# Seven-product output projection: combinations, row transfers and next-layer splits placed step by step, a third pair of split weights

## Chip, cores and metric

One core of one Trainium2 chip runs the whole program. The metric is the device time of one execution in microseconds (us), as a median over runs; lower is better.

## What is computed

A decoder trunk of two layers on 512 positions and 2048 channels, in float32. Each layer normalises x, projects it by `w_in` into the inputs of three groups (a state-space group, a convolution group, a differential attention), gates their outputs and projects them back:

```python
y = jnp.concatenate([y_ssd, y_cfm, y_att], axis=-1)
x = x + jnp.einsum("bse,ed->bsd", y, w_out[l])
```

The change lies in the second line of each layer, in how `x` is handed to the next layer, and in the buffers that serve both.

## The kernel before

Every large matmul is made of three on numbers that are split in two: a weight tile `w` of 128 x 1024 is copied by ACT into a short format (`wh`, line 141) and DVE subtracts that from `w` (`wl`, line 142); activations are split likewise into hi and lo. TensorE then adds hi*wh, hi*wl and lo*wh into a PSUM bank. `weights` (line 130) does this for each weight tile. The pool `wsp` holds two pairs of `wh` and `wl`, so the split of a tile waits until TensorE has ended with the tile two before it.

The output projection of a layer has two halves. Output channels 0 to 1023 come from two calls of `project` (line 815), 8 weight tiles each, 24 matmuls to a tile. Output channels 1024 to 2047 come from seven products (`product`, line 859), a scheme that saves the eighth product of a 2 x 2 split of the matrices and pays with sums: of activations (`s_make`, line 788, done before), of weights (`w_add` and `w_less`, lines 846 and 854, one DVE instruction of 128 x 1024 to a tile), and of results (`each`, line 890, DVE instructions of 128 x 512).

Each product has four **steps**; this text numbers them 0 to 27 in a layer, so product 1 is steps 0 to 3 and product 7 steps 24 to 27. A step loads one weight tile of 512 KB by SP (`load`, line 831: four buffers in turn, two of the pool `wraw` and the tags `vA` and `vB`), sums it into one of four running tiles `wsum` where the product asks for a sum (products 2, 3, 5 and 7), splits it and runs 12 matmuls of 512 columns. The results of a product lie in two PSUM tiles: `pa` (products 1 and 6), `pc` (2 and 4), `pb` (3, 5 and 7).

The four groups of output rows `r22`, `r12`, `r21` and `r11`, two tiles of 128 x 512 each, start as rows of x that POOL loads from memory (`x_rows`, line 885), and gather the products: r22 takes p1 (a copy of `pa` after product 1, line 928), `pc` after product 2 and `pb` after product 5; r12 takes p1, `pb` after product 3 and `pc` after product 4; r21 takes p1 and, last, `pb` after product 7; r11 takes `pa` after product 6. `done` (line 908) stores them.

In the first layer the next layer's activations are made beside the products. Channels 0 to 1023 of the new x are read back from memory by `again` (line 915: POOL loads, eight tiles of 256 KB); the rows of the products are transposed by TensorE and copied by ACT (`turn`, line 897). `put_x` (line 120) then scales and splits a tile (ACT line 117, DVE line 118) and adds its square to a running sum for the normalisation (ACT lines 110 and 113, DVE line 114).

TensorE's order is the order in which the program is written. The order on ACT, DVE, SP and POOL is set by a scheduler at build time, by priority: what stands in `with urgent()` goes before everything, `soon()` before the rest, and `with tc.issue_after(ins)` keeps an instruction behind `ins`. In the kernel before, the weight splits, the sums of weights and the combinations (`each`) are all urgent, and the squares of `again`'s tiles are put wherever the scheduler finds room. On the chip each engine takes its instructions strictly in the order that was so made, and so do the DMA queues.

Of the kernel before, what the change touches and what calls it, by code (L numbers as in the profile page):

```python
# [45 lines left out]
def kernel(  # L46
# [83 lines left out]
    def weights(src, raw=None, between=None):  # L130

        with urgent():
# [3 lines left out]
            h = wsp.tile([P, 2, S], F32R, tag="wh", name="wh")  # L136
            lo = wsp.tile([P, 2, S], F32R, tag="wl", name="wl")
# [92 lines left out]
    def load_x(kk, w):  # L230
# [7 lines left out]
        for j in range(2):  # L238
            k = 2 * kk + j
            if k in (8, 10):  # L240
                xv[0] = big.tile([P, 2, S], F32, tag=("vA", "vB")[(k - 8) // 2], name=f"xraw{k}")
            t = xv[0][:, k % 2, :] if 8 <= k < 12 else big.tile([P, S], F32, tag=f"xs{k}" if k < 8 else f"p{k - 12}", name=f"xraw{k}")
# [30 lines left out]
    for l in range(DEPTH):  # L273
# [43 lines left out]
        else:  # L317
            jobs = late + [lambda: after(1, x_stats), par_load, lam_job]
# [78 lines left out]
        xs = [None] * 8  # L397
# [79 lines left out]
        def conv_x(i, raws, xs=xs, conv4=conv4):  # L477
            xs[i] = big.tile([P, S], F32, tag=f"xs{i}", name=f"xs{i}")
            conv4(raws[i % 4], i, xs[i])
# [245 lines left out]
        def ssd_out(i, xs=xs, ry=ry, yact=yact, col=col, yv=yv):  # L725
            t = wt2()
            V.scalar_tensor_tensor(t, xs[i], col(PP_SN + i), ry[0], ALU.mult, ALU.mult)
            if i in (0, 2):
                yv[0] = big.tile([P, 2, S], F32R, tag=("vA", "vB")[i // 2], name=f"ysh{i}")
            hi = yv[0][:, i % 2, :] if i < 4 else big.tile([P, S], F32R, tag=f"p{i - 4}", name=f"ysh{i}")  # L730
            lo = big.tile([P, S], F32R, tag=f"xs{i}", name=f"ysl{i}")
            split(hi, lo, t)
            yact[i] = (hi, lo)
# [37 lines left out]
        banks = in_proj(CH_CZ, True, mix([ahead(lambda t=t: att_out(t)) for t in range(4)] + [lambda i=i: ssd_out(i) for i in range(8)],  # L771
# [82 lines left out]
        def w_less(s_):  # L854
            raw = load(quarter(0, 0, s_))
            V.tensor_tensor(raw, chain[s_], raw, ALU.subtract)
            return raw

        def product(src, lhs, banks, start, jobs=()):
# [35 lines left out]
        xk = [None] * KB  # L895

        def turn(t, e, c, xk=xk):
# [4 lines left out]
            for b in range(4):  # L902
                k = 8 + 4 * e + b
                if xk[k] is None:
                    xk[k] = big.tile([P, S], F32, tag=f"p{b}", name=f"x1_{k}") if e else rw()
                A.copy(xk[k][:, blk(t)], ps[:, blk(b)])

        def done(tiles, t0, e, l=l):
# [4 lines left out]
            return [lambda n=n: turn(t0 + n, e, tiles[n]) for n in range(2)] if l < DEPTH - 1 else []  # L913
# [5 lines left out]
        nxt = l < DEPTH - 1  # L919
        put = lambda *ks, l=l, xk=xk: [lambda k=k: put_x(l + 1, k, xk[k]) for k in ks] if nxt else []  # L920
        r21 = x_rows([lt([P, S], "rl"), lt([P, S], "rc")], 2, 0)
# [12 lines left out]
        each(ALU.add, r21, r21, p1)  # L934
        product(w_add(1, 1), lambda j, t: part(slab(8 + j), 2 + t), pb, True,
                [lambda k=k: again(k) for k in range(4, 8)] if nxt else [])
        each(ALU.subtract, r12, r12, pb)
        r11 = x_rows([wt2(), wt2()], 0, 0)
        product(lambda s_: load(quarter(1, 1, s_)), lambda j, t: part(slab(j), 2 + t), pc, False)
        each(ALU.subtract, r12, r12, pc)  # L940
        jobs = done(r12, 0, 1)
        product(w_less, lambda j, t: part(slab(j), t), pb, False, [lambda: None] * 2 + jobs)
        each(ALU.subtract, r22, r22, pb)
        jobs = done(r22, 2, 1)
        product(lambda s_: load(quarter(1, 0, s_)), lambda j, t: part(yact[k1(j)], t), pa, False,
                [lambda: None] * 2 + jobs + put(0, 1, 2, 3))
        each(ALU.add, r11, r11, pa)
        jobs = done(r11, 0, 0)
        product(w_add(1, 0), lambda j, t: part(yact[k1(j)], 2 + t), pb, False,
                [lambda: None] * 2 + jobs + put(4, 5, 6, 7))  # L950
        each(ALU.add, r21, r21, pb)
        jobs = done(r21, 2, 0)
# [71 lines left out]
```

## Time and profile before

| what | value |
|---|---|
| median of 3 runs | 1555.08 us (1554.63 to 1555.27) |
| the profiled execution's own time | 1558.73 us |
| its span, first to last instruction | 1557.0 us |
| TensorE (PE) busy | 1530.3 us, 98% |
| DVE busy | 1121.7 us, 72% |
| ACT busy | 747.5 us, 48% |
| POOL busy | 72.8 us, 5% |
| mean granted TensorE clock | 0.996 |

The profiled execution is 3.65 us above the median of the runs. "Busy" of PE counts a matmul until its modelled end, so PE is nearly always busy in it; what a stretch of matmuls loses shows in their starts, which follow each other at a constant pace as long as nothing is waited for.

### The profile page before, as it was taken

Reading aid. Unit: us, or ns where it says so; the run is one execution under the profiler, and the core shown is the slowest. Engines: PE = TensorE matmul, PEld = TensorE weight load, DVE = VectorE, ACT = ScalarE, POOL = GpSimd, SP = SyncE. Lnnn points to the kernel's source line nnn. Section 1 sums busy time; section 2 is a strip of 40 time slices with the busy share of each in tenths; the row PEclk is TensorE's granted clock in tenths of the full one; section 3 lists DMA queues with packets and bytes.
Section 4 is the critical chain, followed back from the end, with each engine's and each line's share of the span. In section 5 each row is a group of like instructions: output and inputs, shape, how many; then the busy total and the mean of one; then the engine's idle time right before and its main releaser. Section 6 shows DMA issues by size and latency. Waiting matters only on the chain.

```text
span 1557.0 us, 18864 instructions
## 1 busy us (share of the span) xinstructions
PE 1530.3 (98%) x7156; PEld 1244.8 (80%) x7156; DVE 1121.7 (72%) x1741; ACT 747.5 (48%) x1173; POOL 72.8 (5%) x136
## 2 busy tenths in 40 slices
PE   9999999999999999998999999999999999999988
PEld 6778888888888888876677788888888888888866
DVE  7654646988688889837856546469886888898475
ACT  6433727333475556323645328273334755563232
POOL 0010100000000000111000101100000000000000
PEclk9999999999999999998999999999999999999999
DMA  7253443333322333445632534332333223345455
GB/s 243 82 144 89 119 118 100 87 97 93 95 81 77 114 118 119 149 159 174 211 101 82 141 92 119 118 100 82 95 95 95 81 74 108 121 118 159 162 158 157
DMA packets 55196, 184.10 MB, mean 118 GB/s; under 512 B 7776, under 2 KB 8672, under 8 KB 55104
## 3 DMA queue, kind: packets, MB, share of 16 engines
q1 hardware_dynamic: 46112, 156.34, 33.2%
q0 software_dynamic: 8992, 26.55, 5.6%
q8 instruction: 56, 0.92, 0.2%
q14 instruction: 36, 0.29, 0.1%
HBM read 174.40 MB, written 8.45 MB: 117 GB/s over the span
## 4 chain that ended last, share of the span: by engine, by line
PE 87%; DVE 4%; DMA 4%; issue 3%; ACT 1%; POOL 1%; SPq 0%; DVEq 0%; POOLq 0%; ACTq 0%
PE ps_p L190 17%; PE ps_p L192 17%; PE ps_p L191 17%; PE ps_p L196 7%; PE ps_p L194 7%; PE ps_p L195 7%; DVE wl L142 2%; DMA wraw<-w_out 2%; PE ps_p L874 2%; PE ps_p L875 2%; PE ps_p L873 1%; PE ps_s L678 1%; PE ps_s L465 1%; PE ps_s L470 1%; DMA e<-acr 1%
## 5 line engine op out<-in xcount | busy, mean ns | idle before, releaser
L141 ACT ACTIVATE wh<-wraw 128x1024 fp32r<-128x1024 f32 (+1 forms) x249 | 262.3, 1054 | 545.7 <-PE ps_p L191 260.9
L142 DVE TENSOR_TENSOR wl<-wraw,wh 128x1024 fp32r<-128x1024 f32 (+1 forms) x249 | 303.1, 1217 | 225.6 <-ACT wh L141 214.5
L190 PE MATMUL ps_p<-xh,wh 128*128 128x512 f32 x1024 | 413.0, 403 | 4.2 <-DVE rw L330 2.7
L192 PE MATMUL ps_p<-xh,wl 128*128 128x512 f32 x1024 | 400.8, 391 | 0.0
L191 PE MATMUL ps_p<-xl,wh 128*128 128x512 f32 x1024 | 399.9, 391 | 0.0
L190 PEld LDWEIGHTS ps_p<-xh,wh 128*128 128x128 f32 x1024 | 193.1, 189 | 53.9 <-ACT wh L141 5.5
L191 PEld LDWEIGHTS ps_p<-xl,wh 128*128 128x128 f32 x1024 | 193.2, 189 | 41.7 <-issue 3.8
L192 PEld LDWEIGHTS ps_p<-xh,wl 128*128 128x128 f32 x1024 | 192.8, 188 | 41.9 <-DVE wl L142 0.3
L194 PE MATMUL ps_p<-wh,xh 128*128 128x512 f32 x512 | 202.6, 396 | 0.0
L196 PE MATMUL ps_p<-wh,xl 128*128 128x512 f32 x512 | 199.7, 390 | 0.0
L195 PE MATMUL ps_p<-wl,xh 128*128 128x512 f32 x512 | 199.4, 389 | 0.0
L519 DVE SCALAR_TENSOR_TENSOR ca<-u,ppt,ca 128x512 f32<-128x512 f32 x240 | 179.3, 748 | 3.5
L196 PEld LDWEIGHTS ps_p<-wh,xl 128*128 128x128 f32 x512 | 96.1, 188 | 20.4
L194 PEld LDWEIGHTS ps_p<-wh,xh 128*128 128x128 f32 x512 | 96.2, 188 | 19.0
L195 PEld LDWEIGHTS ps_p<-wl,xh 128*128 128x128 f32 x512 | 96.3, 188 | 18.9
L141 ACT ACTIVATE wh<-wsum 128x1024 fp32r<-128x1024 f32 x32 | 34.0, 1061 | 67.7 <-PE ps_p L875 22.3
L142 DVE TENSOR_TENSOR wl<-wsum,wh 128x1024 fp32r<-128x1024 f32 x32 | 39.1, 1222 | 16.5 <-ACT wh L141 16.2
L190 PE MATMUL ps_p<-ysh,wh 128*128 128x512 f32 x128 | 50.8, 396 | 0.0
L191 PE MATMUL ps_p<-ysl,wh 128*128 128x512 f32 x128 | 49.9, 390 | 0.0
L192 PE MATMUL ps_p<-ysh,wl 128*128 128x512 f32 x128 | 49.9, 389 | 0.0
L420 DVE TENSOR_TENSOR xdt<-ps_s,dt 128x512 f32<-128x512 f32 x16 | 11.0, 689 | 45.4 <-PE ps_s L418 45.4
L651 DVE TENSOR_TENSOR ps_s<-ps_s,cst 128x128 f32<-128x128 f32 x64 | 18.3, 295 | 34.7 <-PE ps_s L650 34.3
(529 smaller groups left out, 2219.4 us busy)
## 6 DMA issues: line engine op xcount, KB each, us to landing
wraw<-w_in SPq DMA_DIRECT2D x191, 512.0 KB, 3.6
wraw<-w_out SPq DMA_DIRECT2D x80, 512.0 KB, 3.7
m<-acr POOLq DMA_DIRECT2D x32, 256.0 KB, 4.5
xraw<-xT SPq DMA_DIRECT2D x16, 256.0 KB, 5.0
wsum<-w_out SPq DMA_DIRECT2D x8, 512.0 KB, 3.6
out<-rw SPq DMA_DIRECT2D x12, 256.0 KB, 4.1
wT<-acr POOLq DMA_DIRECT2D x24, 96.0 KB, 4.0
rw<-xT POOLq DMA_DIRECT2D x8, 256.0 KB, 4.2
```

Source lines behind the costliest of these rows:

```text
L141: pace_hi[0] = A.activation(h[:, part, :], raw[:, part, :], AF.Copy).ins
L142: pace[0] = V.tensor_tensor(lo[:, part, :], raw[:, part, :], h[:, part, :].bitcast(F32), ALU.subtract).ins
L190: T.matmul(banks[b], h[:, c], ah, start=first, stop=False)
L191: T.matmul(banks[b], h[:, c], al, start=False, stop=False)
L192: T.matmul(banks[b], lo[:, c], ah, start=False, stop=last)
L194: T.matmul(banks[b], ah[:, c], h, start=first, stop=False)
L195: T.matmul(banks[b], ah[:, c], lo, start=False, stop=False)
L196: T.matmul(banks[b], al[:, c], h, start=False, stop=last)
L519: V.scalar_tensor_tensor(ca[i], u[i][:, j:j + S], w(j), ca[i], ALU.mult, ALU.add)
L651: V.tensor_tensor(ps[:, d0:n], ps[:, d0:n], amask, ALU.add)
L874: T.matmul(banks[t], hi, wl, start=False, stop=False, **again)
L875: T.matmul(banks[t], lo, h, start=False, stop=s_ == 3 and j == 1, **again)
```

## The change

`weights` may place its pair in a third pair of buffers: the tags `xs0` and `xs1`, which hold two tiles of 128 x 512 each now (the eight tags `xs0` to `xs7` become four twice as large, and the code that uses them takes them in pairs: `load_x`, `conv_x`, `ssd_out`, `again`). From step 5 on, every third step uses it, so that a split then waits for the tile three before it. `load` and its four raw buffers are not touched.

The combinations, the row loads, the copy of p1, the transposes and the next layer's splits become jobs of a step. A combination is no longer urgent; it stands behind the newest weight split (`paced`). A sum of weights stands behind the split of two steps before (`before[-2]`). The rows r22 and r12 go into the tags `p0` to `p3` instead of `rw`; the ones that are turned into channels 1536 to 2047 go into `rw` and the others into `p0` to `p3`. Of channels 0 to 1023, tiles 0 to 3 are still put beside the products, tiles 4 to 7 only in the next layer's first projection.

```diff
-    def weights(src, raw=None, between=None):
+    def weights(src, raw=None, between=None, third=False):
...
-            h = wsp.tile([P, 2, S], F32R, tag="wh", name="wh")
-            lo = wsp.tile([P, 2, S], F32R, tag="wl", name="wl")
+            h, lo = [big.tile([P, 2, S], F32R, tag=t3, name=n) if third else wsp.tile([P, 2, S], F32R, tag=n, name=n)
+                     for n, t3 in (("wh", "xs0"), ("wl", "xs1"))]
...
                 raw = load(quarter(q, e, s_))
-                V.tensor_tensor(chain[s_], chain[s_], raw, ALU.add)
+                with tc.issue_after(before[-2]):
+                    V.tensor_tensor(chain[s_], chain[s_], raw, ALU.add)
...
-                wt = weights(None, raw)
+                wt = weights(None, raw, third=steps[0] > 4 and steps[0] % 3 == 2)
+                steps[0] += 1
+                before.append(pace[0])
...
-        def each(op, dst, a, b):
-            with urgent():
-                for n in range(2):
-                    V.tensor_tensor(dst[n], a[n], b[n], op)
+        def each(op, dst, b):
+            for n in range(2):
+                V.tensor_tensor(dst[n], dst[n], b[n], op)
...
-            xk[k] = big.tile([P, S], F32, tag=f"xs{k}", name=f"x1_{k}")
-            G.dma_start(out=xk[k], in_=x1[k])
+            xp = big.tile([P, 2, S], F32, tag=f"xs{(2, 3, 0, 1)[k // 2]}", name=f"x1_{k}")
+            for n in range(2):
+                xk[k + n] = xp[:, n, :]
+                G.dma_start(out=xp[:, n, :], in_=x1[k + n])
...
-        r22 = x_rows([rw(), rw()], 2, 1)
-        r12 = x_rows([rw(), rw()], 0, 1)
-        p1 = [wt2(), wt2()]
-        with urgent():
-            for n in range(2):
-                A.copy(p1[n], pa[n])
-        each(ALU.subtract, r22, r22, p1)
-        product(w_add(0, 1), lambda j, t: part(slab(8 + j), t), pc, True,
-                [lambda k=k: again(k) for k in range(4)] if nxt else [])
-        each(ALU.subtract, r22, r22, pc)
-        each(ALU.subtract, r12, r12, p1)
-        each(ALU.add, r21, r21, p1)
...
+        product(w_add(0, 1), lambda j, t: part(slab(8 + j), t), pc, True, [
+            lambda: rows_in("22", lambda: [ptile(0), ptile(1)], 2, 1), p1_copy, none, op(SUB, "22", "p")])
+        product(w_add(1, 1), lambda j, t: part(slab(8 + j), 2 + t), pb, True, [
+            op(SUB, "22", pc), none, lambda: rows_in("12", lambda: [ptile(2), ptile(3)], 0, 1), none])
+        product(lambda s_: load(quarter(1, 1, s_)), lambda j, t: part(slab(j), 2 + t), pc, False, [
+            op(SUB, "12", pb), op(SUB, "12", "p"), op(ADD, "21", "p"), none])
+        product(w_less, lambda j, t: part(slab(j), t), pb, False, [
+            seq(op(SUB, "12", pc), lambda: done(rows["12"], 0, 1)),
+            lambda: rows_in("11", lambda: [wt2(), wt2()], 0, 0), *turns("12", 0, 1)])
+        product(lambda s_: load(quarter(1, 0, s_)), lambda j, t: part(yact[k1(j)], t), pa, False, [
+            seq(op(SUB, "22", pb), lambda: done(rows["22"], 2, 1), only(lambda: (again(0), again(2)))),
+            none, seq(*turns("22", 2, 1)), only(later(lambda: put(0, 1)))])
+        product(w_add(1, 0), lambda j, t: part(yact[k1(j)], 2 + t), pb, False, [
+            seq(op(ADD, "11", pa), lambda: done(rows["11"], 0, 0)), only(later(lambda: put(2, 3))),
+            *turns("11", 0, 0)])
...
+            late = [lambda again=again: (again(4), again(6)),
+                    lambda tn=tn, put=put: (tn[0](), tn[1](), put(4, 5)),
...
```

What this makes of the order on the engines is shown at three places, all in the first layer. In them `wsum` and `wraw` are the weight tiles that are summed or split, `wl` and `wh` the split pair, `rb` and `sa` the running sum of squares and one square, `x_0` to `x_7` the tiles that `again` reads back, `wT` the copy of p1. Before, DVE's order from the split of step 3 to the combinations ahead of the split of step 7 is:

```order
L142 TENSOR_TENSOR wl<-wsum,wh 128x1024
L114 TENSOR_TENSOR rb<-rb,sa 128x512
L849 TENSOR_TENSOR wsum<-wsum,wraw 128x1024
L142 TENSOR_TENSOR wl<-wsum,wh 128x1024
L893 TENSOR_TENSOR rl<-rl,wT 128x512
L849 TENSOR_TENSOR wsum<-wsum,wraw 128x1024
L893 TENSOR_TENSOR rc<-rc,wT 128x512
L142 TENSOR_TENSOR wl<-wsum,wh 128x1024
L114 TENSOR_TENSOR rb<-rb,sa 128x512
L893 TENSOR_TENSOR rw<-rw,wT 128x512 x2
L142 TENSOR_TENSOR wl<-wsum,wh 128x1024
L893 TENSOR_TENSOR rw<-rw,wT 128x512 x2
```

After the change DVE's order from the split of step 3 through that of step 9 is:

```order
L142 TENSOR_TENSOR wl<-wsum,wh 128x1024
L855 TENSOR_TENSOR wsum<-wsum,wraw 128x1024
L142 TENSOR_TENSOR wl<-wsum,wh 128x1024 x2
L855 TENSOR_TENSOR wsum<-wsum,wraw 128x1024 x2
L142 TENSOR_TENSOR wl<-wsum,wh 128x1024 x2
L855 TENSOR_TENSOR wsum<-wsum,wraw 128x1024 x2
L903 TENSOR_TENSOR rows<-rows,wT 128x512
L142 TENSOR_TENSOR wl<-wsum,wh 128x1024
L855 TENSOR_TENSOR wsum<-wsum,wraw 128x1024
L142 TENSOR_TENSOR wl<-wsum,wh 128x1024
```

All four combinations with the rows that are loaded in product 2 (`rw` before) stood ahead of the splits of steps 6 and 7; now one (`rows`) stands ahead of the split of step 8, and the sums of weights stand two at a time ahead of two splits. ACT's order before, from the splits of steps 0 to 2 on:

```order
L141 ACTIVATE wh<-wsum 128x1024 x3
L110 ACTIVATE rb<-x_0_5710 128x512
L113 ACTIVATE sa<-x_1_5731 128x512
L141 ACTIVATE wh<-wsum 128x1024
L113 ACTIVATE sa<-x_2_5752 128x512
L113 ACTIVATE sa<-x_3_5773 128x512
L141 ACTIVATE wh<-wsum 128x1024
```

and after the change, from the splits of steps 0 to 5 on (`x_0_6039` holds tiles 0 and 1, `x_2_6042` tiles 2 and 3):

```order
L141 ACTIVATE wh<-wsum 128x1024 x6
L950 COPY wT<-ps_p 128x512 x2
L110 ACTIVATE rb<-x_0_6039 128x512
L113 ACTIVATE sa<-x_0_6039 128x512
L141 ACTIVATE wh<-wsum 128x1024 x2
L113 ACTIVATE sa<-x_2_6042 128x512 x2
L141 ACTIVATE wh<-wsum 128x1024 x4
```

The first two squares moved from ahead of the split of step 3 to ahead of the split of step 6, the next two to ahead of the split of step 8, and the squares of tiles 4 to 7 are gone from here. At the end of the first layer's products DVE's order after the change, from the last combination to the split for the second weight tile of the next layer's first projection, is:

```order
L903 TENSOR_TENSOR rl<-rl,ps_p 128x512
L502 MEMSET u_7689 128x30
L118 SCALAR_TENSOR_TENSOR xl_122<-rw,nwt,xh_106 128x512
L903 TENSOR_TENSOR rc<-rc,ps_p 128x512
L502 MEMSET u_7692 128x30
L118 SCALAR_TENSOR_TENSOR xl_113<-x_6_6283,nwt,xh_97 128x512
L142 TENSOR_TENSOR wl<-wraw,wh 128x1024
```

The split of tile 6 of the new x, read back into the buffers of the third pair, now stands ahead of that weight split. On all engines the instructions ahead of the first layer's products, and between the next layer's first projection and its products, stand in the order of before, apart from the names of buffers.

## Rows read from the trace of the kernel before

**Rows 1.** Windows: busy us (and instructions) of PE, PEld, DVE, ACT, POOL; clock, DMA.

```profile
690.00:789.00 99.00, 88.03 (x371) 68.11 (x370) 76.93 (x86) 48.53 (x79) 12.01 (x23) 0.95 0.57 188
1468.00:1553.00 85.00, 79.15 (x338) 62.34 (x336) 60.93 (x61) 29.71 (x29) 3.22 (x6) 1.00 0.58 182
...
717.30:722.80 5.50, 5.50 (x13) 4.34 (x14) 4.46 (x5) 0.49 (x1) 1.07 (x2) 0.50 0.49 141
```

**Rows 2.** Waits of PE: total us, times, longest.

```profile
PE ps_s L874 <- DVE wl L142: 7.8, 5, 3.5
PE ps_p L874 <- DVE wl L142: 5.9, 8, 1.7
```

**Rows 3.** Timeline of PE (start, us): ends of both layers' products, end of product 1.

```profile
690.24 0.40 PE L873 MATMUL ps_p<-wh,ysh 128*128 128x512 f32 x1
...
788.76 0.40 PE L190 MATMUL ps_p<-xh,wh 128*128 128x512 f32 x1
...
1468.12 0.40 PE L873 MATMUL ps_p<-wh,ysh 128*128 128x512 f32 x1
...
1478.81 0.39 PE L875 MATMUL ps_p<-wh,ysl 128*128 128x512 f32 x1
...
1552.28 0.40 PE L875 MATMUL ps_p<-wh,ycl 128*128 128x512 f32 x1
```

**Rows 4.** Timeline of PE, first layer: other work between the products' matmuls.

```profile
706.75 1.07 PE L269 MATMUL ps_s<-rw,wd 128*32 128x512 f32 x8
...
758.48 0.60 PE L901 MATMUL ps_s<-cst,rw 128*128 128x128 f32 x4
758.84 0.48 PE L873 MATMUL ps_p<-wh,xh 128*128 128x512 f32 x1
```

**Rows 5.** Timeline of PE, first layer: the two longest waits.

```profile
701.30 0.50 PE L873 MATMUL ps_p<-wh,ysh 128*128 128x512 f32 x1 [2.70 <-ACT wh L141]
...
717.21 0.80 PE L874 MATMUL ps_s<-wl,xh 128*128 128x512 f32 x1 [3.50 <-DVE wl L142]
```

**Rows 6.** Timeline of ACT, first layer, ahead of the wait at 701.30.

```profile
697.21 0.63 ACT L110 ACTIVATE rb<-x 128x512 f32<-128x512 f32 x1 [2.95 <-DMA x<-x]
699.67 0.63 ACT L113 ACTIVATE sa<-x 128x512 f32<-128x512 f32 x1 [1.83 <-DMA x<-x]
700.20 1.04 ACT L141 ACTIVATE wh<-wsum 128x1024 fp32r<-128x1024 f32 x1
```

**Rows 7.** Timeline of POOL, then of DVE, first layer, ahead of the wait at 717.21.

```profile
708.09 2.12 POOL L887 DMA_DIRECT2D rw<-xr  x4 [0.44 <-PE ps_s L269]
...
714.68 1.34 DVE L893 TENSOR_TENSOR rw<-rw,wT 128x512 f32<-128x512 f32 x2 [4.42 <-issue]
```

**Rows 8.** Timeline of DVE, second layer, steps 4 to 6.

```profile
1478.37 1.23 DVE L849 TENSOR_TENSOR wsum<-wsum,wraw 128x1024 f32<-128x1024 f32 x1 [2.25 <-DMA wraw<-w_out]
...
1480.64 1.89 DVE L893 TENSOR_TENSOR rw<-rw,wT 128x512 f32<-128x512 f32 x3
...
1483.05 1.22 DVE L142 TENSOR_TENSOR wl<-wsum,wh 128x1024 fp32r<-128x1024 f32 x1
```

**Rows 9.** Landing: lines L838 and L917; weight loads issued in 685:720 and 1466:1490.

```profile
DMA to landing us min/median/max: 3.4/4.0/8.9
...
DMA to landing us min/median/max: 3.0/6.2/6.6
...
wraw<-w_out SPq DMA_DIRECT2D x7, 512.0 KB, 6.4
...
wraw<-w_out SPq DMA_DIRECT2D x8, 512.0 KB, 5.2
```

**Rows 10.** Durations (page's groups: busy us, mean ns, idle before; line L849: ns).

```profile
L141 ACT ACTIVATE wh<-wsum 128x1024 fp32r<-128x1024 f32 x32 | 34.0, 1061 | 67.7 <-PE ps_p L875 22.3
L142 DVE TENSOR_TENSOR wl<-wsum,wh 128x1024 fp32r<-128x1024 f32 x32 | 39.1, 1222 | 16.5 <-ACT wh L141 16.2
...
L849 DVE TENSOR_TENSOR wsum<-wsum,wraw x24: 1218/1222/1227, 687.5 to 1543.2; 128x1024 f32<-128x1024 f32 x24
```

More of the change, by code (lines that the diff above doesn't have):

```diff
@@ L317 @@
         else:
-            jobs = late + [lambda: after(1, x_stats), par_load, lam_job]
+            jobs = late + [lambda: (after(1, x_stats), par_load()), lam_job]
         banks = in_proj(CH_BC, True, jobs, first_pre, order=range(KB // 2) if l == 0 else KORD)
@@ L769 @@
             yact[12 + h] = (yah[:, h, :], yal[:, h, :])
-        banks = in_proj(CH_CZ, True, mix([ahead(lambda t=t: att_out(t)) for t in range(4)] + [lambda i=i: ssd_out(i) for i in range(8)],
+        banks = in_proj(CH_CZ, True, mix([ahead(lambda t=t: att_out(t)) for t in range(4)] + [(lambda i=i: ssd_out(i)) if i % 2 == 0 else (lambda: None) for i in range(8)],
                                          tp[6] + [cfm_norm] + [lambda: None] * NPAD))
@@ L855, in w_less @@
             raw = load(quarter(0, 0, s_))
-            V.tensor_tensor(raw, chain[s_], raw, ALU.subtract)
+            with tc.issue_after(before[-2]):
+                V.tensor_tensor(raw, chain[s_], raw, ALU.subtract)
             return raw
+        before, steps = [], [0]
         def product(src, lhs, banks, start, jobs=()):
@@ L888, in x_rows @@
             return tiles
-        def each(op, dst, a, b):
-            with urgent():
-                for n in range(2):
-                    V.tensor_tensor(dst[n], a[n], b[n], op)
+        def each(op, dst, b):
+            for n in range(2):
+                V.tensor_tensor(dst[n], dst[n], b[n], op)
         xk = [None] * KB
+        nxt = l < DEPTH - 1
         def turn(t, e, c, xk=xk):
@@ L904, in turn @@
                 if xk[k] is None:
-                    xk[k] = big.tile([P, S], F32, tag=f"p{b}", name=f"x1_{k}") if e else rw()
-                A.copy(xk[k][:, blk(t)], ps[:, blk(b)])
+                    xk[k] = rw() if e else big.tile([P, S], F32, tag=f"p{b}", name=f"x1_{k}")
+                with tc.issue_after(pace_hi[0]):
+                    A.copy(xk[k][:, blk(t)], ps[:, blk(b)])
         def done(tiles, t0, e, l=l):
@@ L933 @@
-        each(ALU.subtract, r12, r12, p1)
-        each(ALU.add, r21, r21, p1)
[L935 to L952, printed above, removed]
@@ L953 @@
-        if nxt:
-            both = lambda a, b: lambda: (a(), b())
-            pt = put(12, 13, 14, 15, 8, 9, 10, 11)
-            late = [both(pt[0], pt[1]), both(pt[2], pt[3])] + jobs + [
-                lambda xk=xk: (dt_mm(3, xk[12:16], 2), dt_mm(2, xk[8:12], 2)), both(pt[4], pt[5]), both(pt[6], pt[7])]
+            xp = big.tile([P, 2, S], F32, tag=f"xs{(2, 3, 0, 1)[k // 2]}", name=f"x1_{k}")
+            for n in range(2):
+                xk[k + n] = xp[:, n, :]
+                G.dma_start(out=xp[:, n, :], in_=x1[k + n])
@@ new lines, in put, with rows_in, p1_copy @@
+        def put(*ks, l=l, xk=xk):
+            for k in ks:
+                put_x(l + 1, k, xk[k])
+        ptile = lambda n: big.tile([P, S], F32, tag=f"p{n}", name="rows")
+        none = lambda: None
+        later = lambda fn: lambda: paced(fn)
+        only = lambda fn: fn if nxt else none
+        rows = {}
+        def rows_in(key, tiles, t0, e):
+            rows[key] = x_rows(tiles(), t0, e)
+        def p1_copy():
+            rows["p"] = [wt2(), wt2()]
+            with tc.issue_after(pace_hi[0]):
+                for n in range(2):
+                    A.copy(rows["p"][n], pa[n])
@@ new lines @@
+        op = lambda o, key, b: later(lambda: each(o, rows[key], rows[b] if isinstance(b, str) else b))
+        SUB, ADD = ALU.subtract, ALU.add
+        turns = lambda key, t0, e: [only(lambda n=n: turn(t0 + n, e, rows[key][n])) for n in range(2)]
+        seq = lambda *fns: lambda: [fn() for fn in fns]
+        rows_in("21", lambda: [lt([P, S], "rl"), lt([P, S], "rc")], 2, 0)
+        product(w_first, lambda j, t: part(yact[j], t), pa, True, jobs)
+        product(w_add(0, 1), lambda j, t: part(slab(8 + j), t), pc, True, [
+            lambda: rows_in("22", lambda: [ptile(0), ptile(1)], 2, 1), p1_copy, none, op(SUB, "22", "p")])
@@ new lines @@
+        with urgent():
+            each(ADD, rows["21"], pb)
+        done(rows["21"], 2, 0)
+        if nxt:
+            tn = turns("21", 2, 0)
+            late = [lambda again=again: (again(4), again(6)),
+                    lambda tn=tn, put=put: (tn[0](), tn[1](), put(4, 5)),
+                    lambda put=put: put(6, 7, 12, 13), lambda put=put: put(14, 15),
+                    lambda put=put, xk=xk: (dt_mm(3, xk[12:16], 2), dt_mm(2, xk[8:12], 2), put(8, 9)),
+                    lambda put=put: put(10, 11)]
```

32 lines of the change are left out of this document (15 added, 17 removed).

## The prediction

> **What bounds the kernel now.** I read the windows of the two stages first, then the waits of PE, then the starts of its matmuls, and then ACT and DVE ahead of the longest waits. TensorE is the bound nearly everywhere, so a change is worth what it takes out of the time that TensorE loses, and only the two stretches of the seven products are touched in order.
>
> What is lost there follows from starts. In product 1 of the second layer nothing is waited for: from 1468.12 to 1478.81 there are 47 starts, a pace of 0.2274 us [rows 3]. The second layer's products have 335 further starts up to 1552.28, in 84.16 us; at that pace they would take 76.2, so 8.0 us are lost. The first layer's take 98.52 us from 690.24 to the next projection's first matmul at 788.76. Of this 336 starts are 76.4; the eight small matmuls for the next layer's `dt` cost 1.1 and six groups of four transposes 0.36 each, or 2.2 [rows 4]. That leaves 18.8 us lost, and **26.8 us in both layers**.
>
> The waits of PE say where. Most are for `wl`, the DVE half of a weight split: 7.8 and 5.9 us, in 5 and 8 waits [rows 2], and one of 2.70 us for `wh`, the ACT half [rows 5]. The two longest show what an order in advance does to an engine that can't pass anything:
> - Ahead of 701.30 ACT stands at two squares of tiles that are just being read back: 2.95 and 1.83 us idle, released by DMA. The weight split behind them starts at 700.20, and PE, which needs it, has been waiting [rows 6].
> - Ahead of 717.21 POOL issues the row loads at 708.09, and DVE stands 4.42 us at the combination that wants them. What released it is given as issue, but the rows land only then; the weight splits of steps 6 and 7 stand behind [rows 7].
>
> After both, TensorE runs at half clock for a while: 13 matmuls in 5.50 us at a granted 0.50, that is 1.2 GHz, where 13 x 0.2274 = 3.0 would do at 2.4, so 2.5 us more [rows 1]. In the second layer the clock is 1.00 throughout [rows 1] and the same mechanism is short: a sum waits 2.25 us for its weights, then four combinations run ahead of a split [rows 8].
>
> **The change, part by part.**
>
> *Third pair and fixed places.* No arithmetic is added: DVE keeps its 28 splits and 16 sums of 1.22 us and 18 combinations of about 0.69 in each layer [rows 8, 10]. With two pairs a split (1.06 on ACT and 1.22 on DVE, [rows 10]) has one step, 12 x 0.2274 = 2.73 us, between the end of the matmuls that free its buffer and the ones that want it, so a sum of 1.22 beside it leaves 0.3, and any combination makes PE wait. With three pairs it has two steps, 5.46. Since a combination now stands at most one or two at a time between splits, and at a place where its product has ended, all waits behind combinations go, if nothing new comes. I follow the steps in the order that DVE has now and find slack of 2 us or more in products 4 to 7. Products 2 and 3 are the tight ones, since the third pair begins only at step 5 and the loads crowd there.
>
> *Step 6, first layer.* Product 1 begins at 690.24 as before, step 2 ends at 698.4, the product at 701.15, the eight small matmuls at 702.2; so step 6 begins at 707.7 and step 8 at 713.1. Two things gate the split of step 6. On ACT the squares of tiles 0 and 1 now stand ahead of it: their loads go into buffers that step 2 frees, at 698.4, behind two row loads at 0.53 each [rows 7], so about 699.4; landing took 3.0 to 6.6, median 6.2 [rows 9], and I take the median, since eight loads still go together: 705.6. A square (0.63, [rows 6]), the ACT half and the DVE half bring 708.5, with hand-overs 708.8. On DVE the sum of step 7 stands ahead: its load is issued at the end of the sum of step 5, near 699.6, lands 6.4 later (the median of this crowded stretch, [rows 9]) at 706.0, and sum and split make 708.5. PE wants `wl` at 707.9, so it waits **1.0**. Bounds: 0 with a landing of 4.0, 3.4 with one of 8.9 [rows 9].
>
> *Step 8, first layer.* The load of step 9 is issued at 707.3, lands by 712.5 (5.2, as in the second layer's crowd, [rows 9]); sum, one combination and the split end at 715.6, PE wants it at 714.3: **1.3**.
>
> *Second layer.* There are no squares. The sum of step 5 ends near 1477.3; load, sum of step 7 and split of step 6 end at 1477.4 + 5.2 + 1.22 + 1.22 = 1485.1, wanted at 1484.7: **0.4**. The same for steps 9 and 8: 1491.5 against 1490.6: **0.9**.
>
> *Row loads and copies.* r22 and r12 go into buffers that product 1 frees, up to ten us earlier than before, and their combinations stand behind splits; p1's copy stands behind the split of step 5 on ACT. Both are covered by the 5.46 us. If that cover were gone they would cost 0.69 each.
>
> *End of the first layer.* Tiles 4 to 7 are read into the third pair's buffers once step 26 has ended, and the split of the next projection's second weight tile stands behind tile 6. From the end of step 26 to its use there are 0.36 + 2.73 + 0.36 for step 27 and transposes, 24 x 0.2274 = 5.46 for the first tile and 0.23: 9.1. The chain is a landing of 6.2, at most 1.06 on ACT for the tile, then 1.06 and 1.22 for the weights: 9.5, so **0.3** to 0.4; 0 with a landing of 3.0, 0.8 with 6.6. The squares and scalings that moved there lie beside projection steps of 5.46 us and cost nothing; without that cover they would be 0.6 to 0.7 a tile.
>
> *The sum.* 26.8 go, 1.0 + 1.3 + 0.4 + 0.9 + 0.3 = 3.9 remain or come new: 22.9 us less. Against the profiled execution's own 1558.73 this is 1535.8; it stands 3.65 above the median of the runs, so the median becomes 1555.08 - 22.9 = **1532**. With nothing left over it would be 1528.
>
> **A rule that speaks against it.** The loads that matter went from 4.0 us (median of all weight loads of the products) to 8.9 where POOL's and SP's go together [rows 9]. The Trainium skill, "DMA: Bandwidth & Descriptors", section "Issuing engines are not separate DMA queues", says that transfers run on the same 16 DMA engines and interleave whichever engine started them. The trace agrees (8.9 against 4.0), and by that rule the row loads, now moved to the start of product 2, would lengthen the weight loads that the splits wait for; what this would give is the first rival.
>
> **The rivals.**
>
> *A: the crowd stays.* Weight loads of product 2 land in 8.9 us, as the slowest did. First layer: the load of step 7 lands at 708.7, the split of step 6 ends at 711.3, a wait of 3.4, long enough for the half clock (2.5 more); step 8 adds about 1.8. Second layer: 1477.4 + 8.9 + 2.4 = 1488.7, a wait of 4.0, again 2.5, and 2.1 at step 8. With 0.3 at the end 16.6 stay, 10.2 go: **1545**. For it: the same number of loads lies in the same 15 us. Against: they are issued further apart, and 8.9 was the slowest of 48.
>
> *B: DVE becomes the bound in the first layer.* It has 44 x 1.22 + 18 x 0.69 = 66 us there, and about ten splits and sums of the next layer's tiles, of 0.7 each, 73 in all, beside 79.7 of TensorE. If DVE stands idle as long as before, 99.0 - 76.9 = 22.1 us [rows 1], the stage takes 95 instead of 98.5, and only the second layer's 8.0 and these 3.5 go: **1544**. Against: the idle time was waiting for what now stands behind splits. Nearly the same follows if the change does less than its words: `load` is not in the diff, so the two raw buffers are not new, and should the third pair help no split, the second layer keeps its 8.0 and the first some 4 more, 1540.
>
> *C: slower.* A raw buffer is given back only by its sum, and sums now have a fixed place behind the split of two steps before, where they went as soon as their weights were there. If every load took 8.9 instead of 4.0, each of the two chained loads in products 5 and 7 would come 4.9 later with about 2 covered: 2 x 2.9 x 4 products = 23, on top of A's 16.6, 40 lost instead of 26.8: **1568**. It decides from a landing near 7 us in all products. Against: half of the loads land within 4.0 [rows 9].
>
> *N: the waits return elsewhere in full*, 1555. Nothing in the order shows where.
>
> **How the numbers follow.** The forecast (1528 to 1540: 1532 with the bounds of the waits, 0 to 3.4 at step 6 with its slow clock, less at the others) has 0.76, A 0.10, B 0.07, N 0.03, C 0.04. The range from 1528 to 1541 leaves out A, N, C and part of B, 2 in 10. 0.2% is 3.1 us, about what a measurement of this kernel can tell from no change: faster 0.93, same 0.03, slower 0.04.
>
> **What would show it.** In the changed profile the second layer's products should take 77 to 78 us instead of 84.2, the first layer's 82 to 84 instead of 98.5, with a granted clock of 1.00 in both; the waits of PE for `wl` in the products should fall from 13.7 to some 4 us, those left at steps 6 and 8, behind a weight load or, on ACT, behind a square. It is wrong if the clock still falls to 0.50 in the first layer (A), if DVE is busy without a gap while PE waits (B), if DVE stands at sums waiting for `wraw` in products 5 and 7 (C), or if the next layer's first projection waits for more than 1 us.

## The result, and the profile after

The changed kernel takes **1534.38 us** (median of 4 runs, 1534.10 to 1534.66), the kernel before beside it 1555.17: a ratio of 0.9864, 95% interval 0.9847 to 0.9882, 20.8 us less. A second measurement gave 1535.06 and 0.9868 (0.9847 to 0.9888). Forecast were 1532 and a range of 1528 to 1541.

Windows of the two stages of products, in the columns of [rows 1]; they are now 81.89 and 77.22 us long, so the windows are too:

```profile
689.00:772.00 83.00, 82.04 (x374) 66.30 (x374) 70.40 (x78) 41.25 (x63) 12.49 (x24) 1.00 0.67 224
1450.00:1528.00 78.00, 77.33 (x340) 63.23 (x338) 61.35 (x62) 29.63 (x29) 3.23 (x6) 1.00 0.62 197
```

The clock is 1.00 in both. In the first stage DVE is idle for 12.6 us (83.00 - 70.40) instead of 22.1 (99.00 - 76.93), and busy for 6.5 us less than in [rows 1]: the squares and splits of tiles 4 to 7 have left the stage. In the second stage its work is about the same, 61 us. The waits of PE over the whole span, to be held against [rows 2]:

```profile
PE ps_p L190 <- DVE rw L330: 2.9, 4, 1.0
PE ps_p L190 <- ACT wh L141: 1.7, 1, 1.7
PE ps_s L219 <- DVE sa L215: 1.5, 1, 1.5
PE ps_s L885 <- DVE wl L142: 1.4, 2, 0.8
PE ps_s L884 <- ACT wh L141: 0.2, 1, 0.2
```

The products (lines 884 to 886) wait 1.6 us where they waited 16.4 (7.8 + 5.9 + 2.7); the other three lines lie elsewhere in the program. The starts that bound the stages, in the timeline of PE, answer to [rows 3]:

```profile
689.05 0.40 PE L884 MATMUL ps_p<-wh,ysh 128*128 128x512 f32 x1
...
770.94 0.48 PE L190 MATMUL ps_p<-xh,wh 128*128 128x512 f32 x1
...
1450.54 0.40 PE L884 MATMUL ps_p<-wh,ysh 128*128 128x512 f32 x1
...
1527.76 0.40 PE L886 MATMUL ps_p<-wh,ycl 128*128 128x512 f32 x1
```

Between the profiled executions the difference is 1558.73 - 1534.10 = 24.6 us: 98.52 - 81.89 = 16.6 in the first layer's products, 84.16 - 77.22 = 6.9 in the second's, 1.2 ahead of the first (690.24 against 689.05), and -0.1 in the rest. Whether the 1.2 is the change's stays open: in the profiled executions of the kernel before and its variants the products start at 689.9 to 690.3, in those of the changed kernel and its variants at 688.7 to 690.5. Of the loss 2.2 (81.89 - 79.7) and 1.0 (77.22 - 76.2) are left, 1.4 and 0.8 of it in step 6 of each layer; most of the rest of the first layer lies in starts that come 0.1 late behind the transposes and the small matmuls. Timeline of the first layer, ACT, DVE and PE:

```profile
704.84 0.63 ACT L110 ACTIVATE rb<-x 128x512 f32<-128x512 f32 x1 [4.08 <-DMA x<-x]
705.38 0.62 ACT L113 ACTIVATE sa<-x 128x512 f32<-128x512 f32 x1
705.90 1.99 ACT L141 ACTIVATE wh<-wsum 128x1024 fp32r<-128x1024 f32 x2
...
704.82 1.23 DVE L855 TENSOR_TENSOR wsum<-wsum,wraw 128x1024 f32<-128x1024 f32 x1 [2.03 <-DMA wraw<-w_out]
706.97 2.36 DVE L142 TENSOR_TENSOR wl<-wsum,wh 128x1024 fp32r<-128x1024 f32 x2 [0.92 <-ACT wh L141]
...
706.99 0.50 PE L884 MATMUL ps_s<-wh,xh 128*128 128x512 f32 x1 [0.20 <-ACT wh L141]
708.25 0.50 PE L885 MATMUL ps_s<-wl,xh 128*128 128x512 f32 x1 [0.76 <-DVE wl L142]
```

ACT stands at a square until tile 0 has landed, DVE at a sum until its load has; the square decides, by 0.92 us. The two starts of PE cost 1.4 us. In the second layer the sum alone does it, and costs 0.8:

```profile
1465.54 1.23 DVE L855 TENSOR_TENSOR wsum<-wsum,wraw 128x1024 f32<-128x1024 f32 x1 [1.71 <-DMA wraw<-w_out]
...
1467.96 0.50 PE L885 MATMUL ps_s<-wl,xh 128*128 128x512 f32 x1 [0.67 <-DVE wl L142]
```

### The profile page after: what moved, and what is told of

The parts are those of the page before. It is cut to its first block, busy times and chain, and to the rows that moved or that the text cites. A ratio compares the mean times of both kernels' runs of the same rounds, so it can differ in the third digit from the quotient of the medians.

```text
span 1532.3 us, 18840 instructions
## 1 busy us (share of the span) xinstructions
PE 1520.2 (99%) x7156; PEld 1241.8 (81%) x7156; DVE 1121.0 (73%) x1741; ACT 747.1 (49%) x1173; POOL 73.0 (5%) x136
## 4 chain that ended last, share of the span: by engine, by line
PE 91%; DMA 3%; issue 2%; DVE 2%; ACT 1%; POOL 1%; SPq 0%; ACTq 0%; POOLq 0%
PE ps_p L190 18%; PE ps_p L192 17%; PE ps_p L191 17%; PE ps_p L196 7%; PE ps_p L194 7%; PE ps_p L195 7%; PE ps_p L884 2%; PE ps_p L885 2%; PE ps_p L886 2%; PE ps_s L680 1%; PE ps_s L465 1%; PE ps_s L470 1%; DMA e<-acr 1%; PE ps_s L885 1%; PE ps_s L886 1%
## 5 line engine op out<-in xcount | busy, mean ns | idle before, releaser
L142 DVE TENSOR_TENSOR wl<-wsum,wh 128x1024 fp32r<-128x1024 f32 x32 | 38.9, 1222 | 16.6 <-ACT wh L141 16.5
```

The lines of the kernel that those rows point to most:

```text
L142: pace[0] = V.tensor_tensor(lo[:, part, :], raw[:, part, :], h[:, part, :].bitcast(F32), ALU.subtract).ins
```

## The experiments

In this table "first" is the time from product 1's first matmul to the next projection's first, 79.7 where nothing is lost, "second" that from the first to the last matmul of the second layer's products, 76.2. They come from the starts of PE in the one profiled execution, the median from all runs, the ratio is to the kernel before on the same chip. The chips differ: on three of them the kernel before had a median of 1554.29 to 1555.20, so medians of different rows compare to about 1 us, and the ratios are the safer measure. "Places" are the fixed places of sums, combinations and the copy of p1.

| kernel | median | ratio (95%) | first | second |
|---|---|---|---|---|
| before, second profile | 1555.14 (1 run) | | 95.9 | 83.3 |
| changed, again | 1535.06 | 0.9868 (0.9847-0.9888) | 82.4 | 77.6 |
| changed, two pairs only | 1539.67 | 0.9904 (0.9889-0.9919) | 84.4 | 77.7 |
| changed, third pair without places | 1536.21 | 0.9887 (0.9872-0.9901) | 83.1 | 79.1 |
| changed, neither of the two | 1550.96 | 0.9973 (0.9961-0.9985) | 88.3 | 84.8 |
| changed, combinations first | 1537.56 | 0.9893 (0.9878-0.9908) | 83.7 | 78.3 |
| changed, sums free | 1536.01 | 0.9882 (0.9866-0.9899) | 83.3 | 78.1 |
| before, early row loads | 1554.60 | 0.9994 (0.9983-1.0004) | 91.5 | 86.7 |
| before, late squares | 1554.63 | 0.9997 (0.9982-1.0011) | 94.6 | 83.4 |
| before, both | 1559.38 | 1.0021 (1.0011-1.0032) | 97.5 | 87.0 |
| changed, read-back tiles held | 1534.12 | 0.9863 (0.9845-0.9881) | 81.4 | 76.6 |
| changed, tiles and r12 held | 1534.41 | 0.9862 (0.9843-0.9882) | 81.2 | 77.0 |

### Is it the third pair or the places?

Two pairs, places kept:

```diff
-                wt = weights(None, raw, third=steps[0] > 4 and steps[0] % 3 == 2)
+                wt = weights(None, raw, third=False)
...
-                G.dma_start(out=xp[:, n, :], in_=x1[k + n])
+                if k < 4:
+                    G.dma_start(out=xp[:, n, :], in_=x1[k + n])
+                else:
+                    with tc.issue_after(pool[0]):
+                        G.dma_start(out=xp[:, n, :], in_=x1[k + n])
```

(`pool[0]` is the newest store of rows.)

> The changed kernel with all its places, but every split in one of the two old pairs; tiles 4 to 7 of the new x are still read back only behind the last row store of the first layer. My theory (places and third pair both needed): a split again has one step of 2.73 us between the end of the matmuls that free its pair and its use, of which the two halves take 2.5; beside a split DVE has room for one sum and 0.3 us, so each sum with a combination beside it costs 0.4 to 0.7, some 6 to 9 such in a layer. The second layer's products lose 4 to 6 us instead of 1.0, the first layer's 6 to 8 instead of 2.2, the whole 1541 to 1546. Rival (the places did it all, the third pair is idle): 1534 to 1536. Rival (the third pair did it all, the places are idle): the old 8.0 in the second layer, 1550 or more.

1539.67: under the range of my theory, far from both rivals. The second layer's products lose 1.5 us, not 4 to 6. Not all of the difference to the changed kernel is the third pair's. In the changed kernel the loads of tiles 4 to 7 are issued ahead of the last two row stores, at 767.57 us, and not, as the text above has it, behind them; with this edit they come at 775.52. Their splits pile up ahead of a weight split in the next layer's first projection, and PE, which never waits for one there in the changed kernel, has lost 1.0 us to that kernel by then. In the timeline of PE:

```profile
798.35 0.50 PE L192 MATMUL ps_p<-xh,wl 128*128 128x512 f32 x1 [0.77 <-DVE wl L142]
```

Why the second layer loses so little shows in the timeline of DVE in its product 3:

```profile
1479.49 1.22 DVE L142 TENSOR_TENSOR wl<-wsum,wh 128x1024 fp32r<-128x1024 f32 x1
1480.63 1.21 DVE L855 TENSOR_TENSOR wsum<-wsum,wraw 128x1024 f32<-128x1024 f32 x1
1481.77 0.67 DVE L903 TENSOR_TENSOR rows<-rows,ps_s 128x512 f32<-128x512 f32 x1
1482.37 1.21 DVE L142 TENSOR_TENSOR wl<-wsum,wh 128x1024 fp32r<-128x1024 f32 x1
```

From split to split a sum and a combination take 2.88 us, not the 3.1 that the three durations add up to: each instruction starts about 0.07 before the end of the one ahead of it. That is 0.15 over the pace of 2.73 a step, where I had counted 0.4 to 0.7.

The third pair, places taken away:

```diff
-                with tc.issue_after(before[-2]):
-                    V.tensor_tensor(chain[s_], chain[s_], raw, ALU.add)
+                V.tensor_tensor(chain[s_], chain[s_], raw, ALU.add)
...
-        op = lambda o, key, b: later(lambda: each(o, rows[key], rows[b] if isinstance(b, str) else b))
+        op = lambda o, key, b: now(lambda: each(o, rows[key], rows[b] if isinstance(b, str) else b))
```

(`now` runs its function in `urgent()`; `w_less` and the copy of p1 likewise.)

> The changed kernel with the third pair, but sums, combinations and the copy of p1 put where the scheduler finds them ready first, ahead of other work, as in the kernel before. My theory: with two steps for a split a combination of 0.69 or a sum ahead of it is covered as long as none of them waits for a transfer; the scheduler now puts combinations one at a time. Second layer loses 1 to 3 us, first 3 to 6: 1536 to 1541. Rival (the places did it all): the losses of before come back, 1550 or more. Rival (the third pair did it all): 1534 to 1535.

1536.21, as my theory had it, at its lower end, and not far from the second rival's 1535. One wait of 1.8 us for `wl` in product 7 of the second layer is the largest piece. So either of the two, beside the rest of the change, brings most of the gain. The third pair in the kernel before, with nothing else changed, was not tried. Both edits together leave what else the change does, rows loaded early, squares late:

> The changed kernel without its third pair and without its places: two pairs, and sums, combinations and the copy of p1 put where the scheduler finds them ready first. What stays of the change: the rows r22 and r12 are loaded into buffers that are free ten us earlier, squares of tiles 4 to 7 and their loads lie behind the products, those of tiles 0 to 3 later in them. Theory 1 (after the runs with one of the two taken away, which lost only 2 to 5 us: places and third pair stand in for each other, and with neither all is lost): 1548 to 1553, the second layer's products lose 6 to 8 us. Theory 2 (the gain lies in what no longer waits for a transfer, that is in the row loads and squares): 1538 to 1543, and the second layer's products lose 2 to 4.

1550.96, Theory 1. Its waits of PE, in the products only:

```profile
PE ps_s L883 <- DVE wl L142: 7.2, 6, 3.4
PE ps_p L883 <- DVE wl L142: 3.7, 5, 1.9
```

The second layer loses 8.6 us, as much as before (8.0, and 7.1 in its second profile, the first row of the table). What else the change does is worth 0.27% by itself (0.15 to 0.39), about 4 us; no run shows which part of it does that. The four corners: without the places the third pair is worth 1550.96 - 1536.21 = 14.8 us, with them 1539.67 - 1534.38 = 5.3, of which about 1 lies at the late tiles, by the profiled execution; the places are worth 11.3 without the third pair, 1.8 with it. By the ratios the four are 0.9%, 0.4%, 0.7% and 0.2%, and for the last the two intervals overlap: that it is above zero is not shown by them. They stand in for each other: the one gives a split more time, the other takes work from ahead of it.

Two single places. The combinations `urgent` again, the rest as changed (only the `op` line of the diff above):

> The changed kernel, only the combinations put first again as in the kernel before; sums keep their place, third pair kept. My theory: two combinations and two sums at a time come ahead of two splits (2 x 0.69 + 2 x 1.22 = 3.8 us in a row), which two steps of 2.73 still cover where the data has landed; 1535 to 1539, the difference in products 2 and 3 of both layers. Rival (fixed places of the combinations carry most of the gain): 1545 or more.

1537.56, within my range, far from the rival, and in product 3 where expected: it takes 11.9 us in both layers against 10.65. The sums without their place (the other lines of that diff):

> The changed kernel, only the sums of weights without their place behind the split of two steps before. My theory: sums go earlier where their load has landed by the scheduler's estimate, later loads are issued earlier, but a sum that stands ahead of a split and waits for its load holds that split; 1534 to 1538. The rival of the prediction that the fixed place of the sums makes loads late would see this kernel faster: 1531 to 1533.

1536.01, within my range. It is not faster, so the prediction's rival of late loads behind fixed sums has no support.

### Do the two long waits alone explain it?

Three edits of the kernel before. The first loads r22 and r12 into free buffers:

```diff
-        r22 = x_rows([rw(), rw()], 2, 1)
-        r12 = x_rows([rw(), rw()], 0, 1)
+        r22 = x_rows([ptile(0), ptile(1)], 2, 1)
+        r12 = x_rows([ptile(2), ptile(3)], 0, 1)
...
-                    xk[k] = big.tile([P, S], F32, tag=f"p{b}", name=f"x1_{k}") if e else rw()
+                    xk[k] = rw() if e else big.tile([P, S], F32, tag=f"p{b}", name=f"x1_{k}")
```

> The kernel before; only the rows r22 and r12 are loaded into the buffers that product 1 frees, and the turned tiles change places with them. Two pairs, no places. Theory 2: the wait of 3.50 us in product 2 of the first layer goes with its 2.5 at half clock, and of the second layer's 8.0 the 2.8 of product 2: 1546 to 1549. Theory 1: the combinations still stand four at a time ahead of splits; no more than 2 us, 1553 to 1555.

1554.60, no change. The wait it aimed at did go: product 2 of the first layer takes 11.0 us from its first to its last start, before 17.2 and in the second profile 15.5. But in the second layer it takes 15.4, before 13.4 and 12.5. Timeline there, DVE and PE:

```profile
1473.91 0.69 DVE L893 TENSOR_TENSOR rows<-rows,wT 128x512 f32<-128x512 f32 x1 [1.53 <-DMA rows<-x1t]
1474.52 0.69 DVE L893 TENSOR_TENSOR rl<-rl,wT 128x512 f32<-128x512 f32 x1
1475.12 0.69 DVE L893 TENSOR_TENSOR rows<-rows,wT 128x512 f32<-128x512 f32 x1
1475.73 1.22 DVE L849 TENSOR_TENSOR wsum<-wsum,wraw 128x1024 f32<-128x1024 f32 x1
1476.86 1.22 DVE L142 TENSOR_TENSOR wl<-wsum,wh 128x1024 fp32r<-128x1024 f32 x1
...
1478.14 0.80 PE L874 MATMUL ps_s<-wl,xh 128*128 128x512 f32 x1 [2.69 <-DVE wl L142]
```

A row load, three combinations and a sum stand ahead of the split: the same pattern with other members, and after it 3.2 us at half clock (a granted 0.51).

The second puts the scaling and the squares of `put_x` behind the newest split on ACT:

```diff
-        put = lambda *ks, l=l, xk=xk: [lambda k=k: put_x(l + 1, k, xk[k]) for k in ks] if nxt else []
+        def put_held(k, l=l, xk=xk):
+            with tc.issue_after(pace_hi[0]):
+                put_x(l + 1, k, xk[k])
+        put = lambda *ks: [lambda k=k: put_held(k) for k in ks] if nxt else []
```

> The kernel before; only the scaling and squares of the tiles that are read back stand behind the weight split of their step on ACT. Theory 2: the wait of 2.70 us in product 1 of the first layer goes with its 2.5 at half clock, the rest stays: 1549 to 1551. Theory 1: product 1 shortens, but product 2 then waits for the row loads as much longer, 1554 to 1556.

1554.63, no change. Product 1 falls from 16.2 to 10.7 us, and product 7 rises from 13.6 to 17.1, not product 2, where I had looked for it. Timeline at product 7, DVE and PE:

```profile
766.88 1.23 DVE L849 TENSOR_TENSOR wsum<-wsum,wraw 128x1024 f32<-128x1024 f32 x1 [2.33 <-DMA wraw<-w_out]
768.03 0.68 DVE L114 TENSOR_TENSOR rb<-rb,sa 128x512 f32<-128x512 f32 x1
768.63 0.74 DVE L118 SCALAR_TENSOR_TENSOR xl<-x,nwt,xh 128x512 fp32r<-128x512 f32 x1
769.29 0.68 DVE L893 TENSOR_TENSOR wT<-wT,ps_p 128x512 f32<-128x512 f32 x1
769.89 1.22 DVE L142 TENSOR_TENSOR wl<-wsum,wh 128x1024 fp32r<-128x1024 f32 x1
...
771.16 0.50 PE L874 MATMUL ps_p<-wl,yah 128*128 128x512 f32 x1 [3.50 <-DVE wl L142]
```

The squares that no longer hold ACT now stand between a late sum and the split on DVE. With both edits:

> The kernel before with both edits, the early row loads and the squares behind splits; two pairs, no places for sums and combinations. Theory 2: both long waits of the first layer go with their half clock, and a part of the second layer's: 1541 to 1545. Theory 1: 1551 to 1555.

1559.38, slower than before (1.0021, 1.0011 to 1.0032) and outside both theories. Product 2 of the first layer takes 19.4 us. Eight tile loads, four row loads and five weight loads are issued between 692 and 705; one weight load's issue in the DMA view (KB, us to landing), and PE in the timeline:

```profile
wraw<-w_out SPq DMA_DIRECT2D x1, 512.0 KB, 10.4
```

```profile
704.37 0.50 PE L874 MATMUL ps_s<-wl,xh 128*128 128x512 f32 x1 [1.54 <-DVE wl L142]
...
711.39 0.80 PE L874 MATMUL ps_s<-wl,xh 128*128 128x512 f32 x1 [4.01 <-DVE wl L142]
```

10.4 us to land, where the slowest of before took 8.9 [rows 9]: the crowd of the prediction's rival A is real. The changed kernel has four tile loads fewer there.

### What is left at step 6

> The changed kernel once more, as the measure for the two that follow: 1534 to 1535, products 82 and 77 us, the wait at step 6 again 1.0 to 1.7 us in the first layer, behind the square of a tile that lands late, and about 1.0 in the second.

1535.06, stages of 82.4 and 77.6 us, step 6 waiting 0.63 for `wh` and 0.76 for `wl` in the first layer and 1.03 in the second.

The loads that `again` issues go behind the newest row store, which for tiles 0 to 3 is that of r22, and the squares of tiles 0 to 3 go behind the splits:

```diff
-                G.dma_start(out=xp[:, n, :], in_=x1[k + n])
+                with tc.issue_after(pool[0]):
+                    G.dma_start(out=xp[:, n, :], in_=x1[k + n])
...
-            none, seq(*turns("22", 2, 1)), only(later(lambda: put(0, 1)))])
+            none, seq(*turns("22", 2, 1)), only(held(lambda: put(0, 1)))])
```

(`held` is `later` with `tc.issue_after(pace_hi[0])` around it; `put(2, 3)` likewise.) The edit does more than the text put on record ahead of it says: `again` loads tiles 4 to 7 too, and these now go behind the last stores of the layer.

> The changed kernel; the tiles 0 to 3 that are read back are loaded behind the stores of r22, and their scaling and squares stand on ACT behind the weight split of their step. Theory (the wait at step 6 of the first layer has two gates, the square of a late tile on ACT and the sum of step 7 on DVE, whose load lands late in the crowd): both gates go in the first layer, 1.4 us less than the changed kernel, 1532.5 to 1533.5; the second layer's 1.0 stays. Rival (the ACT gate only hides the DVE gate): 0.3 to 0.6 less. Rival (work moved to the end of the layer delays the next projection): no gain.

1534.12. Product 2 of the first layer takes 10.8 us instead of 12.8: no wait is left at step 6. Product 7 takes 12.3 instead of 11.3, with a new wait, in the waits of PE:

```profile
PE ps_p L885 <- DVE wl L142: 0.8, 1, 0.8
```

More is given back in the next layer's first projection. The loads of tiles 4 to 7 are issued at 774.67 us, in the changed kernel at 767.57, and PE waits there for a weight split behind their splits; by then it has lost 1.1 us to the changed kernel's second profile. In the timelines of POOL and PE:

```profile
774.67 2.13 POOL L934 DMA_DIRECT2D x<-x  x4
```

```profile
795.74 0.50 PE L192 MATMUL ps_p<-xh,wl 128*128 128x512 f32 x1 [0.48 <-DVE wl L142]
```

So step 6 lost its wait and a part of the gain went to the next projection, as the last rival had it, and the runs (1533.99 to 1535.60) overlap those of the changed kernel beside it (1534.88 to 1535.38): no gain that these runs can tell from none. What holding tiles 0 to 3 alone would gain, with tiles 4 to 7 left in their place, was not run. Then the rows r12 by SP, behind the weight load of step 10:

```diff
-            op(SUB, "22", pc), none, lambda: rows_in("12", lambda: [ptile(2), ptile(3)], 0, 1), none])
+            op(SUB, "22", pc), none, rows_12, none])
...
+        def rows_12():
+            t = rows["12"] = [ptile(2), ptile(3)]
+            with tc.issue_after(newest[0]):
+                for n in range(2):
+                    nc.sync.dma_start(out=t[n], in_=e_in(n, 1))
```

> As the last, and the rows r12 come by SP behind the weight load of step 10 instead of by POOL at the start of product 2. Theory (what is left at step 6 of the second layer is the load of step 7, which lands in 5.8 us while four row loads are under way, where weight loads alone take 3.6 to 4): the wait there goes as well, 1531 to 1532.5. Rival (the landing is slow for the weight loads' own sake): as held_again.

1534.41, runs from 1532.78 to 1535.83: inconclusive. Tiles 4 to 7 are late here too (773.65). The second layer's wait at step 6 is gone, but it was gone in the last kernel too, which changes nothing there. What differed is the landing of the load of step 7, in the DMA view 6.2 us in the changed kernel's second profile and 4.8 in the kernel with tiles held:

```profile
wraw<-w_out SPq DMA_DIRECT2D x1, 512.0 KB, 6.2
```

```profile
wraw<-w_out SPq DMA_DIRECT2D x1, 512.0 KB, 4.8
```

With the row loads in the same place it differs by 1.4 us from execution to execution. Whether r12's move helps stays open.

### How much of before's loss is one execution's

> The kernel before, one more look, because its runs spread over 6 us and its profiled execution stood 3.65 above the median. Theory (a wait of 2.7 or 3.5 us is followed by half clock in some executions and not in others, 2.5 us each): the waits for weight splits are again 16 to 17 us in sum, and the time differs by the number of stretches at half clock, 0, 1 or 2. Rival (the waits themselves differ from run to run): the sum of waits differs by 2 us or more at the same clock.

1555.14. Waits of PE in the products, and a window of the clock behind the second long wait, to be held against [rows 2] and [rows 1]:

```profile
PE ps_p L874 <- DVE wl L142: 5.8, 8, 1.1
PE ps_s L874 <- DVE wl L142: 5.3, 5, 2.8
...
PE ps_p L873 <- ACT wh L141: 2.6, 1, 2.6
```

```profile
716.30:719.80 3.50, 3.50 (x10) 2.72 (x11) 3.50 (x5) 0.00 (x0) 1.07 (x2) 0.58 0.32 98
```

The waits are 13.7 us instead of 16.4, and half clock comes again after both long waits; behind the second it lasts for 8 starts instead of 12. So my theory falls, and the rival holds: 2.7 of the 3.5 us by which the stages differ are waits. The stages are 95.9 and 83.3 us long, and the whole is 3.6 shorter than in the execution shown before.

## Why the prediction was right, point by point

- **What bounds the kernel, and how much is lost.** Right: 26.8 us of the execution shown were lost in the products, 3.2 are left, and nothing else moved but 1.2 us ahead of them, for which no run shows a cause.
- **Third pair and fixed places.** The outcome was right, "all waits behind combinations go". The reason was half right: "a sum of 1.22 beside it leaves 0.3, and any combination makes PE wait" is too dear. With two pairs and the places the second layer lost 1.5 us. Each of the two without the other kept most of the gain.
- **Step 6, first layer.** 1.0 forecast (0.9 by its own times, 708.8 - 707.9), 1.4 measured, with both gates as described. The sum counts one square on ACT where two stand ahead of the split; the second starts 0.54 behind the first. Tile 0 landed in 6.8 us (6.2 taken), the load of step 7 in 6.6 (6.4). The half clock of the bound's upper end did not come.
- **Step 6, second layer.** 0.4 forecast, 0.8 measured: the load landed in 5.8, 5.2 was taken.
- **Step 8.** Wrong: 1.3 and 0.9 forecast, none in either layer. The step that failed is that the load of step 9 "lands by 712.5", in 5.2 us, "as in the second layer's crowd". It was issued at 706.1 instead of 707.3, landed in 4.4 us, and the one after it in 3.7: the crowd was over. I had carried the price of one load over to the next.
- **End of the first layer.** 0.3 forecast, none measured, since the tile landed in 4.2 us instead of the 6.2 taken. Timeline of POOL, ACT and DVE; PE has no wait there:

```profile
767.57 2.14 POOL L931 DMA_DIRECT2D x<-x  x4 [5.47 <-PE ps_p L886]
...
771.82 0.72 ACT L117 ACTIVATE xh<-x,nwt 128x512 fp32r<-128x512 f32 x1 [3.06 <-DMA x<-x]
...
773.53 1.23 DVE L142 TENSOR_TENSOR wl<-wraw,wh 128x1024 fp32r<-128x1024 f32 x1 [0.20 <-ACT wh L141]
```

- **The sum.** 22.9 us were to go in the two stages, 23.6 went in the profiled executions (16.6 + 6.9), 20.8 between the medians. The mis-sized step is "so the median becomes 1555.08 - 22.9": the 3.65 us by which the execution shown stood above the median lay nearly all in the stages whose waits the change removes (3.5 of them, by the second profile). They could not go twice. With the second profile's losses, 16.2 + 7.1, the same working gives 1555.1 - 23.3 + 3.9 = 1535.7, and the measurements are 1534.4 and 1535.1.
- **The rivals.** A did not come: the loads that step 6 waits for took 6.6 and 5.8 us, not 8.9 (and by the prediction's own times its wait of 3.4 is 699.6 + 8.9 + 2.4 - 707.9 = 3.0). Its mechanism showed in the kernel before with both edits, 10.4. B: DVE was busy for 70.4 us in the first stage, where 73 were taken, and idle for 12.6. "Should the third pair help no split" came at 1539.67 where 1540 was given, but not by that working: the second layer kept 1.5 us, not 8.0, and about 1 lay in the next projection. C and N had nothing for them.
- **What the prediction did not see.** Its account of the two long waits was true of that execution, but neither wait is a price by itself: the edits that removed them one by one gained nothing, since another late load then found a stack ahead of another split, in step 5 of the second layer and in step 24 of the first.

## What to carry to other kernels

A wait behind a late load in an in-order queue is a symptom. Where a buffer gives a split one step of time, removing one late thing brings the next one forward; give the split a second step, or take the work from ahead of it, and most of the lateness is covered wherever it comes (here all but step 6). Price two remedies for one wait by their four corners, not as a sum. Look in the trace at everything that an edit moved, and not only at what it was meant to move: here tiles that were held by the way cost about 1 us. And before a saving is taken off a median, ask whether the profiled execution's surplus lies in what is saved.

## What the runs showed of the hardware

Half clock behind a long wait is not certain. In the kernel without third pair and places PE waited 3.39 us, and the clock behind it stayed at 1.00 (2.4 GHz); in the kernel before with late squares 3.50 us were followed by a mean of 0.61 over 4.4 us, with 7 starts at half pace (1.2 GHz). Timeline and window of the one, window of the other:

```profile
712.71 0.50 PE L883 MATMUL ps_s<-wl,xh 128*128 128x512 f32 x1 [3.39 <-DVE wl L142]
```

```profile
712.70:718.00 5.30, 5.29 (x23) 4.40 (x24) 4.94 (x5) 1.55 (x2) 0.00 (x0) 1.00 0.52 143
```

```profile
771.10:775.50 4.40, 4.34 (x12) 3.43 (x13) 4.14 (x6) 0.00 (x1) 0.54 (x1) 0.61 0.31 119
```

The length of the wait does not settle it. In the second profile of the kernel before, a wait of 2.75 us ended at 716.24, with 0.58 behind it (its window is shown above). With late squares a wait of the same 2.75 us was followed by 1.00, here and on to 718:

```profile
708.41 0.50 PE L874 MATMUL ps_s<-wl,xh 128*128 128x512 f32 x1 [2.75 <-DVE wl L142]
```

```profile
708.40:711.10 2.70, 2.69 (x12) 2.17 (x12) 2.21 (x3) 0.00 (x0) 0.00 (x0) 1.00 0.81 313
```

The Trainium skill, "TensorE: Matmul & The Clock Gate", section "Part 1: The HAM clock gate (the "warmup" mystery)", says that the number of matmuls at the low clock at the start of a kernel differs between runs of that kernel. The traces show the like in the middle of one: behind the wait in step 6 of the first layer there were 12 starts at half pace in the one execution of the kernel before, 8 in the other, though the waits, 3.50 and 2.75 us, were not alike either.
